# Two unused tiles that move the transposed, gathered and feed-forward rows to other addresses

## The chip, the cores and the metric

The kernel runs on one core of a Trainium2 chip. The metric is the device time of one execution in microseconds (us), as the median of several runs. The engines are named as in the profile: PE is TensorE's matmul, PEld its weight load, DVE is VectorE, ACT is ScalarE, POOL is GpSimd, and SP is SyncE, whose queue issues nearly all loads.

## The reference

The program is a network on one sequence of 256 rows of 1024 numbers, all in float32:

```python
def reference(...):
    x = first_block(x, c, w_ada, ...)
    return second_block(x, positions_2, w_in_2, ...)
```

`first_block` computes a modulation `mod = silu(c) @ w_ada + b_ada`, then `x + g1 * token_mixer(h)` and `x + g2 * relu(h @ w_ff1)**2 @ w_ff2`, where `h` is a normalised and modulated `x`. `token_mixer` multiplies `h` by `w_in` (1024 x 12800), runs retention (4 heads) and dilated attention (12 heads) and merges them with gates and `w_o`. The feed-forward is 4096 wide. `second_block` has two layers. Each one projects `x` by `w_in_2` (1024 x 2488), mixes it (latent attention, mLSTM and a state-space scan), multiplies by `w_out`, and then applies a mixture of 16 experts: `silu(x @ w_gate) * (x @ w_up)` times the share of the expert, times `w_down`, each expert 256 wide.

## The kernel before

Weights come from HBM in chunks of 128 partitions x 1024 numbers (512 KB). A chunk lands in a tile `raw` (or, for experts that are fetched early, `far`). ACT copies it to `whi` in a rounded format (`wsplit`, line 142) and DVE computes the rest, `wlo = raw - whi` (line 145). The activations are split into two parts in the same way. A product is then three matmuls (`mm3`, lines 164 to 168), hi times hi, hi times lo, lo times hi:

```python
def mm3(self, out, l, r, first, last):
    mm = self.nc.tensor.matmul
    mm(out, l[0], r[0], start=first, stop=False)
    mm(out, l[0], r[1], start=False, stop=False)
    mm(out, l[1], r[0], start=False, stop=last)
```

`l` is the operand that is loaded into the array (128 x 128, 512 bytes in each partition), `r` is streamed past it. In the profile each of the three has a row at PEld and one at PE. Two kinds of product matter here.

- Narrow: `proj_tr` loads weights from the ring (`whi`, `wlo`) and streams 256 columns of transposed activations: `h1T` (first block's input), `h2T` (feed-forward input), `rT` (retention's output), `attT`, `xT` (a layer's input).
- Wide: `proj_nat`, `proj_wide` and the experts' `gate_up` and `down` load 128 x 128 pieces of the activations and stream 512 columns of the ring. The activations here are `h1T`, `mT`, `hT`, `xT`, `ffh` (the feed-forward's hidden rows, in blocks of 512), `xg` (the rows that are gathered for the experts) and `ehT` (an expert's hidden rows). In one short stretch at the start of the feed-forward, `fhi` and `flo` from another pool take the place of the ring.

The stages follow each other: modulation and first products (to about 75 us), retention and attention (to about 430), `w_o`, feed-forward (about 475 to 640), and for each layer its mixer and its experts (layer 0's experts from about 800 to 945 us, layer 1's from about 1110 to 1255). The experts run one after another: 24 wide matmuls of gate and up, 12 of down for the expert before, two transposes.

SBUF is laid out by pools, one behind the other in each partition, in the order in which they are opened: `cp` (constants), `ring` (`raw`, `whi`, `wlo`, six of each), `xp` (`x` and the transposed rows `h1T`, `xT`, `mT`, `hT`, `xh`), `sm` (small tiles), and then the pools of a stage, which reuse the room behind `sm`: `pa`/`pr` (retention), `pt` (attention), `pm` (feed-forward: `h2T`, `ffh`, `fhi`, `flo`), `mix` (a layer's mixer), `moe` (experts: `xg`, `ehT`, `far`, `yh`, `PT`). A tile's size in these pools is a multiple of 512 bytes nearly everywhere, so all tiles of a pool have the same remainder modulo 256; behind `moe`'s small `cslot` it changes once more.

Of the kernel before, what the change touches and what calls it, by code (L numbers as in the profile page):

```python
# [10 lines left out]
F32 = mybir.dt.float32  # L11
# [67 lines left out]
class Kern:  # L79
    BANKS = {"mm": "X", "acc": "X", "A": "A", "y": "A", "B": "B", "gu": "B"}  # L80

    def __init__(self, tc, ctx, I, out):
        self.tc, self.nc, self.I, self.out = tc, tc.nc, I, out
        self.ctx = ctx
        self.cp = ctx.enter_context(tc.tile_pool(name="cp", bufs=1))
        self.ring = ctx.enter_context(tc.tile_pool(name="ring", bufs=3))
        self.xp = ctx.enter_context(tc.tile_pool(name="xp", bufs=2))
        self.sm = ctx.enter_context(tc.tile_pool(name="sm", bufs=4))
        self.dp = ctx.enter_context(tc.tile_pool(name="dp", bufs=1, space=DRAM))
        self.n = 0  # L90
        self.pst = None
        self.early = []
        self.gate = self.mark = None
# [2015 lines left out]
```

## Time and profile before

| | us |
|---|---|
| median of 3 runs (1279.0 to 1281.27) | 1281.07 |
| the profiled execution | 1277.76 |
| its span, first to last instruction | 1276.0 |
| PE busy in the span | 1225.8 |
| DVE busy | 954.5 |
| ACT busy | 739.5 |

The profiled execution is one run, and its own time is the one that belongs to the rows below; 1.76 us lie around its span. Matmuls overlap in the records, so the duration of one (about 390 ns for 512 columns) is longer than the time from its start to the next one's start. The second is what a stream costs.

### The profile page before, as it was taken

The page shows a single profiled execution, that of the slowest core. Times are in us where ns is not written, and L with a number is a line of the kernel's source. Part 1 is how long each engine was busy: PE and PEld are TensorE (multiplying, and loading weights), DVE is VectorE, ACT ScalarE, POOL GpSimd, SP SyncE. Part 2 cuts the span into 40 slices and gives each one's busy share as a digit, 9 for nine tenths or more (in the row PEclk, how much of TensorE's full clock was granted, in tenths as well). Part 3 has the DMA queues.
Part 4 walks back from the last instruction along what each step waited for, and adds up shares of the span by engine and source line. Part 5 has one row for each costly group of instructions (what it writes and reads, how often), then busy time and mean ns, then how long its engine had stood idle before and what let it go on. Part 6 is the DMA issues. An engine that isn't in the chain of part 4 may idle for free.

```text
span 1276.0 us, 20435 instructions
## 1 busy us (share of the span) xinstructions
PE 1225.8 (96%) x7528; PEld 1081.3 (85%) x7528; DVE 954.5 (75%) x1647; ACT 739.5 (58%) x1149; POOL 41.1 (3%) x101
## 2 busy tenths in 40 slices
PE   6999999999999999999999999999999999999995
PEld 6888998998999989898888977888879987788884
DVE  6898656565678765555579768899888976889986
ACT  3554344444555654444466663878766756587873
POOL 0000000000000000000010001000001000100000
PEclk8999999999999999999999998999999999899998
DMA  9996564696577556566563522999876342499982
GB/s 283 327 292 199 182 184 146 195 299 199 184 230 255 172 203 197 182 192 188 156 195 106 163 82 75 351 341 350 281 244 218 104 130 70 130 361 339 353 278 93
DMA packets 177170, 271.98 MB, mean 213 GB/s; under 512 B 16363, under 2 KB 109216, under 8 KB 177060
## 3 DMA queue, kind: packets, MB, share of 16 engines
q1 hardware_dynamic: 175252, 265.70, 64.1%
q10 hardware_dynamic: 1296, 3.81, 0.9%
q8 instruction: 61, 1.00, 0.3%
q0 software_dynamic: 512, 1.08, 0.2%
q14 instruction: 49, 0.40, 0.1%
HBM read 268.41 MB, written 2.12 MB: 212 GB/s over the span
## 4 chain that ended last, share of the span: by engine, by line
PE 77%; DVE 11%; DMA 4%; ACT 3%; issue 2%; POOL 1%; SPq 0%; POOLq 0%; ACTq 0%; DVEq 0%
PE ps L167 21%; PE ps L168 21%; PE ps L166 21%; DVE wlo L145 3%; DMA araw<-in_w_ada 2%; PE ps L1652 2%; DVE zc L1178 1%; PE ps L1266 1%; PE ps L1247 1%; DMA raw<-in_w_in 1%; PE ps L1844 1%; DVE ada L384 1%; PE ps L1257 1%; PE ps L1293 1%; PE ps L1814 1%
## 5 line engine op out<-in xcount | busy, mean ns | idle before, releaser
L142 ACT ACTIVATE whi<-raw 128x1024 fp32r<-128x1024 f32 (+3 forms) x348 | 356.6, 1038 | 264.1 <-PE ps L167 152.5
L145 DVE TENSOR_TENSOR wlo<-raw,whi 128x1024 fp32r<-128x1024 f32 x334 | 398.6, 1205 | 147.8 <-ACT whi L142 144.5
L166 PE MATMUL ps<-h1T,whi 128*128 128x256 f32 x576 | 166.4, 289 | 1.7 <-ACT h1T L496 1.7
L167 PE MATMUL ps<-h1T,whi 128*128 128x256 f32 x576 | 165.4, 287 | 0.7 <-DVE h1T L498 0.6
L168 PE MATMUL ps<-h1T,wlo 128*128 128x256 f32 x576 | 165.6, 288 | 0.0
L145 DVE TENSOR_TENSOR wlo<-far,whi 128x1024 fp32r<-128x1024 f32 x100 | 117.9, 1219 | 5.6 <-ACT whi L142 5.4
L142 ACT ACTIVATE whi<-far 128x1024 fp32r<-128x1024 f32 x100 | 103.2, 1056 | 19.2 <-PE ps L168 9.2
L166 PEld LDWEIGHTS ps<-h1T,whi 128*128 128x128 f32 x576 | 111.5, 194 | 3.3 <-ACT h1T L496 2.3
L167 PEld LDWEIGHTS ps<-h1T,whi 128*128 128x128 f32 x576 | 111.7, 194 | 2.2 <-DVE h1T L498 1.4
L168 PEld LDWEIGHTS ps<-h1T,wlo 128*128 128x128 f32 x576 | 111.6, 194 | 0.2 <-DVE wlo L145 0.2
L166 PE MATMUL ps<-whi,xg 128*128 128x512 f32 x256 | 103.7, 405 | 0.0
L167 PE MATMUL ps<-wlo,xg 128*128 128x512 f32 x256 | 101.5, 397 | 0.0
L168 PE MATMUL ps<-whi,xg 128*128 128x512 f32 x256 | 101.4, 396 | 0.0
L384 DVE SCALAR_TENSOR_TENSOR ada<-araw,silu_c,ada 128x512 f32<-128x512 f32 (+1 forms) x88 | 62.4, 713 | 11.8 <-DMA araw<-in_w_ada 9.4
L166 PE MATMUL ps<-h2T,whi 128*128 128x256 f32 x224 | 62.6, 280 | 0.0
L167 PE MATMUL ps<-h2T,whi 128*128 128x256 f32 x224 | 62.6, 279 | 0.0
L168 PE MATMUL ps<-h2T,wlo 128*128 128x256 f32 x224 | 62.5, 279 | 0.0
L168 PEld LDWEIGHTS ps<-whi,xg 128*128 128x128 f32 x256 | 48.1, 188 | 11.3
L167 PEld LDWEIGHTS ps<-wlo,xg 128*128 128x128 f32 x256 | 48.2, 188 | 9.9 <-DVE wlo L145 0.2
L166 PEld LDWEIGHTS ps<-whi,xg 128*128 128x128 f32 x256 | 48.1, 188 | 10.0
L166 PE MATMUL ps<-whi,ffh 128*128 128x512 f32 x128 | 50.7, 396 | 0.0
L167 PE MATMUL ps<-wlo,ffh 128*128 128x512 f32 x128 | 50.6, 396 | 0.0
(513 smaller groups left out, 2878.5 us busy)
## 6 DMA issues: line engine op xcount, KB each, us to landing
raw<-in_w_in SPq DMA_DIRECT2D x124, 512.0 KB, 4.5
raw<-in_w_ff SPq DMA_DIRECT2D x64, 512.0 KB, 3.7
far<-in_w_gate SPq DMA_DIRECT2D x68, 256.0 KB, 5.9
far<-in_w_up SPq DMA_DIRECT2D x68, 256.0 KB, 6.0
araw<-in_w_ada SPq DMA_DIRECT2D x64, 256.0 KB, 5.2
far<-in_w_down SPq DMA_DIRECT2D x32, 512.0 KB, 6.2
raw<-in_w_down SPq DMA_DIRECT2D x32, 512.0 KB, 7.1
raw<-in_w_gate SPq DMA_DIRECT2D x60, 256.0 KB, 5.6
```

Of the source, the lines that this page charges most:

```text
L142: self.nc.scalar.activation(hv, raw, AF.Copy)
L145: self.nc.vector.tensor_sub(lv, raw, hv)
L166: mm(out, l[0], r[0], start=first, stop=False)
L167: mm(out, l[0], r[1], start=False, stop=False)
L168: mm(out, l[1], r[0], start=False, stop=last)
L384: V.scalar_tensor_tensor(acc, raws[k], sc[:, k : k + 1], acc, op0=OP.mult, op1=OP.add)
L1178: V.scalar_tensor_tensor(zc[:, b], xp_[:, i, k : k + 256], cw(k), zc[:, b], op0=OP.mult, op1=OP.add)
L1247: PE.matmul(p[:, t], qT[:, j, t * 128 : t * 128 + 128], kT[:, j], start=True, stop=True)
L1257: PE.transpose(p[:, s, t * 128 : t * 128 + 128], P[:, t, s * 128 : s * 128 + 128], self.ident)
L1266: PE.matmul(p[:, t, j], PTs[j][:, s, t * 128 : t * 128 + 128], v[:, s, h * 64 : h * 64 + 64], start=j == 0 and t == 0 and s == 0, stop=j = ...
L1293: PE.matmul(out(1), Gm[:, 128:256], rhs(full), start=False, stop=False)
L1652: self.nc.tensor.matmul(p[kb // 2][:, kb % 2], xh[i][:, t, kb * 128 : kb * 128 + 128], P[:, t, hf * 256 : hf * 256 + 256], start=t == 0 an ...
```

## The change

Two tiles are added that no instruction writes or reads. They only take room: 48 numbers (192 bytes in each partition) behind the ring, and 56 numbers (224 bytes) in the pool `sm`.

```diff
         self.cp = ctx.enter_context(tc.tile_pool(name="cp", bufs=1))
         self.ring = ctx.enter_context(tc.tile_pool(name="ring", bufs=3))
+        ctx.enter_context(tc.tile_pool(name="line", bufs=1)).tile([128, 48], F32, name="line")
         self.xp = ctx.enter_context(tc.tile_pool(name="xp", bufs=2))
         self.sm = ctx.enter_context(tc.tile_pool(name="sm", bufs=4))
+        self.sm.tile([128, 56], F32, name="line2", tag="line", bufs=1)
         self.dp = ctx.enter_context(tc.tile_pool(name="dp", bufs=1, space=DRAM))
```

On each of the five engines the built program has the same instructions in the same order and with the same waits; only line numbers (two more behind the pads) and addresses differ. These are the addresses that the allocator gives, in bytes within a partition; the remainder modulo 256 is the same for all 128 x 128 pieces of a tile and all blocks of 256 or 512 columns.

| tile | first address before | mod 256 | after | mod 256 |
|---|---|---|---|---|
| `raw`, `whi`, `wlo` (ring) | 27456, 52032, 76608 | 64 | the same | 64 |
| `h1T`, `xT`, `mT`, `hT`, `xh` | 117568 | 64 | 117760 | 0 |
| `x`, `heads`, the first loads of later experts | 101184 | 64 | 101376 | 0 |
| `h2T` | 144480 | 96 | 144896 | 0 |
| `ffh` | 162912 | 96 | 163328 | 0 |
| `fhi`, `flo` | 179296, 191584 | 96 | 179712, 192000 | 0 |
| `rT`, `attT` | 148576, 160864 | 96 | 148992, 161280 | 0 |
| `xg` | 146528 | 96 | 146944 | 0 |
| `araw` (modulation weights) | 171104 | 96 | 171520 | 0 |
| `P` (choice of the gathered rows) | 142432 | 96 | 142848 | 0 |
| `ehT` | 187552 | 160 | 187968 | 64 |
| `far`, `yh` | 191648 | 160 | 192064 | 64 |
| `PT` (experts) | 179360 | 160 | 179776 | 64 |

## Rows read from the trace of the kernel before

**Rows 1.** The page's first part: busy us, share of the span, instructions.

```profile
PE 1225.8 (96%) x7528; PEld 1081.3 (85%) x7528; DVE 954.5 (75%) x1647; ACT 739.5 (58%) x1149; POOL 41.1 (3%) x101
```

**Rows 2.** Windows: length; PE, PEld, DVE, ACT, POOL busy; granted clock; DMA share; GB/s.

```profile
0.00:75.00 75.00, 62.27 (x390) 57.70 (x391) 57.56 (x117) 33.92 (x52) 2.06 (x18) 0.93 0.95 308
480.00:634.00 154.00, 154.00 (x974) 138.16 (x973) 84.49 (x83) 72.79 (x83) 0.00 (x0) 1.00 0.61 184
820.00:900.00 80.00, 80.00 (x354) 64.37 (x353) 74.59 (x79) 64.53 (x79) 0.00 (x0) 1.00 1.03 349
900.00:920.00 20.00, 20.00 (x90) 16.07 (x90) 17.30 (x20) 14.98 (x20) 0.00 (x0) 1.00 0.77 257
```

**Rows 3.** Timeline, PE: start, duration; first and last of 40 in a row.

```profile
312.14 0.39 PE L167 MATMUL ps<-wlo,h1T 128*128 128x512 f32 x1
...
320.98 0.39 PE L167 MATMUL ps<-wlo,h1T 128*128 128x512 f32 x1
```

**Rows 4.** The same, feed-forward's second product, 40 in a row.

```profile
487.24 0.40 PE L167 MATMUL ps<-wlo,ffh 128*128 128x512 f32 x1
...
496.35 0.40 PE L167 MATMUL ps<-wlo,ffh 128*128 128x512 f32 x1
```

**Rows 5.** The same, a narrow product of the first block, 40 in a row.

```profile
349.07 0.28 PE L167 MATMUL ps<-h1T,whi 128*128 128x256 f32 x1
...
353.75 0.28 PE L167 MATMUL ps<-h1T,whi 128*128 128x256 f32 x1
```

**Rows 6.** The same, feed-forward's first product, 40 in a row.

```profile
503.23 0.28 PE L167 MATMUL ps<-h2T,whi 128*128 128x256 f32 x1
...
507.78 0.28 PE L167 MATMUL ps<-h2T,whi 128*128 128x256 f32 x1
```

**Rows 7.** The same, one expert of layer 0, 35 in a row.

```profile
866.24 0.39 PE L167 MATMUL ps<-wlo,xg 128*128 128x512 f32 x1
...
874.17 0.40 PE L168 MATMUL ps<-whi,xg 128*128 128x512 f32 x1
```

**Rows 8.** Groups of PE by form: count, busy us, mean ns of one, idle.

```profile
L167 PE MATMUL ps<-flo,h2T 128*128 128x512 f32 x12 | 4.7, 389 | 0.0
```

**Rows 9.** The same view, one of the three lines of each product.

```profile
L166 PE MATMUL ps<-h1T,whi 128*128 128x256 f32 x576 | 166.4, 289 | 1.7 <-ACT h1T L496 1.7
L168 PE MATMUL ps<-whi,xg 128*128 128x512 f32 x256 | 101.4, 396 | 0.0
L167 PE MATMUL ps<-h2T,whi 128*128 128x256 f32 x224 | 62.6, 279 | 0.0
L167 PE MATMUL ps<-wlo,ffh 128*128 128x512 f32 x128 | 50.6, 396 | 0.0
L168 PE MATMUL ps<-whi,ehT 128*128 128x512 f32 x128 | 50.2, 395 | 0.0
L168 PE MATMUL ps<-whi,h1T 128*128 128x512 f32 x112 | 43.5, 390 | 0.0
L166 PE MATMUL ps<-rT,whi 128*128 128x256 f32 x128 | 36.0, 284 | 0.1
```

**Rows 10.** Timeline, PE, layer 0's mixer: 25 in a row, three shown.

```profile
767.84 0.40 PE L167 MATMUL ps<-wlo,hT 128*128 128x512 f32 x1
...
769.69 0.39 PE L166 MATMUL ps<-whi,hT 128*128 128x512 f32 x1
...
772.86 0.39 PE L168 MATMUL ps<-whi,hT 128*128 128x512 f32 x1
```

**Rows 11.** Groups of DVE by form: count, busy us, mean ns, idle.

```profile
L145 DVE TENSOR_TENSOR wlo<-raw,whi 128x1024 fp32r<-128x1024 f32 x322 | 389.5, 1222 | 147.8 <-ACT whi L142 144.5 <-DMA raw<-in_w_in 1.7 <-issue 0.3
L145 DVE TENSOR_TENSOR wlo<-far,whi 128x1024 fp32r<-128x1024 f32 x100 | 117.9, 1219 | 5.6 <-ACT whi L142 5.4
```

**Rows 12.** Waits of the load queue, 800 to 945 us: total, times, longest.

```profile
SPq L127 <- DVE wlo L145: 29.1, 35, 3.4
```

**Rows 13.** Chain of the first 75 us, shares by line.

```profile
by line: DMA araw<-in_w_ada 18.6%; DMA raw<-in_w_in 10.3%; DVE ada L384 7.7%; PE ps L167 7.0%; DMA raw<-in_p 6.9%; PE ps L166 6.5%; PE ps L168 6.3%; issue 5.2%; DMA c_t<-in_c 5.1%; PE ps L477 4.7%; SPq L127 3.3%; ACT ht L495 2.4%; PE ps L40
```

## The prediction

> **What bounds the kernel now.** The page's first part comes first: TensorE (PE) is busy for 1225.8 of 1276.0 us, and no other engine comes near [rows 1]. An average hides stages, so I cut the span. In the first 75 us PE is busy for 62.27 us while the DMA engines are 95% busy: this stretch waits for transfers. [...]
>
> [...] All the large products are `mm3` matmuls, 512 or 256 columns wide, each with its own weight load. The timeline gives starts; 40 matmuls in a row span 39 spacings.
> - 512 wide, weights from `h1T`, columns from the ring: 8.84 us, so 226.7 ns [rows 3].
> - 512 wide, weights from `ffh`, columns from the ring: 9.11 us, so 233.6 ns (233.3 over longer stretches) [rows 4].
> - 256 wide, weights from the ring, columns from `h1T`: 4.68 us, so 120.0 ns [rows 5].
> - 256 wide, weights from the ring, columns from `h2T`: 4.55 us, so 116.7 ns [rows 6].
>
> The same instruction, the same clock, no waits, and yet two spacings for either width. What differs is the operands' addresses. In the allocator's table `h1T` and the ring both begin 64 bytes past a multiple of 256, while `ffh` and `h2T` begin 96 past one: their two operands stand 32 bytes apart within a 64-byte unit. Equal offsets give 226.7 and 120.0 ns; 32 apart gives 233.3 and 116.7 ns. Equal offsets thus help the wide matmul and hurt the narrow one. An expert (36 wide matmuls in a row, `xg` then `ehT`, 32 or 96 bytes off the ring) has 34 spacings in 7.93 us, 233.2 ns [rows 7]. Two more rows support a relative effect. The tiles `fhi` and `flo` stand at 96 as `h2T` does, so both operands are at 96: their matmuls last 389 ns [rows 8], as those with `h1T` do (390), against 396 with `ffh` [rows 9]. And in layer 0 a run of `hT` matmuls (both at 64) shows the equal-offset stream settling: from 767.84 to 769.69 us eight spacings of 231 ns, then to 772.86 us fourteen of 226.4 [rows 10]. The stream finds the shorter beat after some nine matmuls; streams 32 apart never do.
>
> **The change, part by part.** It adds two tiles that nothing reads or writes. On every engine the same instructions stand in the same order with the same waits; no instruction is added, so the direct cost is nothing. All of it is addresses. After it the ring is still at 64; `h1T`, `h2T`, `xT`, `rT`, `attT`, `mT`, `hT`, `xg`, `ffh` begin at 0, 64 from the ring; `ehT` goes to 64, level with the ring.
>
> The trace has no long stream with operands 64 bytes apart, so that case is bounded from both sides by the two spacings that it does show. I take 64 apart to act as 0 apart. The reason: `xg` and `ffh` (32 below) and `ehT` (96 above) are 128 bytes apart in their distance to the ring, and still last the same (396, 396 and 395 ns [rows 9]), so only the remainder within some small unit counts, and 64 is the smallest unit that fits all rows.
>
> - Experts: 256 x 3 matmuls with `xg` and 128 x 3 with `ehT` [rows 9], which is 36 for each of 32 experts. Two transposes break the stream once per expert. After them I allow 9 spacings at 231 ns [rows 10], a gain of 2.2 each, and 27 that gain 6.5: 195 ns an expert, 6.2 us in all.
> - Feed-forward, second product: 128 x 3 with `ffh` in eight blocks of 48; by the same count 9 x 2.3 + 39 x 6.7 = 281 ns a block, 2.2 us gained.
> - Feed-forward, first product: 224 x 3 with `h2T` go from 116.7 to 120.0: 672 x 3.33 = 2.2 us lost.
> - `rT` (128 x 3 [rows 9]), `attT` (96) and the 128 gather matmuls of line 1652 are of the narrow kind at 32 apart too. 608 x 3.33 = 2.0 us bounds their loss, nothing is the other bound; I take 1.6, as some of them wait for ACT or DVE.
> - `h1T`, `mT`, `hT`, `xT`: 0 apart before, 64 after: no change.
> - Off PE: VectorE's subtraction that reads a raw chunk takes 1222 ns from the ring (offset 64) and 1219 from `far` (160) [rows 11], so I see no cost of an offset there, and price ACT the same way.
>
> Is the gain in the experts covered by something? An expert would need 8.4 us where it needs 8.6. VectorE is busy for 74.59 of 80.00 us in that stretch [rows 2], 93%, which becomes 96%. The transfers: an expert's weights are 3.15 MB, which in 8.4 us are 374 GB/s, above the 349 that the loads reached from 820 to 900 us [rows 2]. But they run ahead: their queue waits for `wlo` to free buffers (29.1 us in 35 waits [rows 12]), and from 900 to 920 us the rate falls to 257 GB/s with PE still full [rows 2]. So I count the gain whole; with that cover gone the experts would stay at their present pace and the sum at -4.6 + 6.2 = 1.6 us lost.
>
> Sum: -6.2 - 2.2 + 2.2 + 1.6 = -4.6 us. The profiled execution took 1277.76 us (span 1276.0), so 1273.2 by its own time. That is 0.36% off; on the median of the runs, 1281.07, it is **1276.5 us**.
>
> [...]
>
> **The rivals.** All use the sums above; "64 apart" is the open quantity.
> 1. *64 apart settles in neither width* (only exactly equal offsets do). Then the narrow matmuls of `h1T` gain: 576 x 3 [rows 9] less some 250 in the transfer-bound first 75 us, 1476 x 3.33 = 4.9 us, and those of `xT` about 0.8. The wide ones that are level now lose: `h1T` and `mT` 432 x 6.7 = 2.9 us, `hT` and `xT` 288 x 3 = 0.9. `xg`, `ffh`, `h2T`, `rT` stay. `ehT` becomes level, but for 12 matmuls between unsettled ones: 9 x 2.2 + 3 x 6.5 = 39 ns an expert, 1.3 us. Net -3.2 us: 1277.9. For it: nothing in the trace shows 64 apart settling.
> 2. *64 apart is best for both* (wide settle, narrow don't). Gains 6.2 + 2.2 + 5.7, no loss: -14.1 us, 1266.9. Against it: wherever the wide ones settle in the trace, the narrow ones do too.
> 3. *64 apart is worst for both; the kernel is slower.* The wide stream does not settle and the narrow ones sit at 120: +3.8 lost on the narrow, +3.8 on the wide ones that are level now, -1.3 for `ehT`: +6.3 us, 1287.4. It turns on one number, the wide spacing at 64 apart: 3.8 - 1.3 = 2.5 us are lost whatever it is, and 1872 wide matmuls that will be 64 apart have a mean spacing of 231.2 ns now (1152 at 233.3, 432 at 226.7, 288 at about 229.7), so the change loses when the new one is above 231.2 - 1.3 = 229.9 ns, about halfway between the two seen.
> 4. *Offsets are not the cause.* Every tile at 96 or 160 also lies high in the partition, far from the ring, and those at 64 lie near it. If distance makes the difference, nothing changes: 1281. For it: distance and offset go together in all the long streams, `fhi` included [rows 8], whose two operands lie near each other. [...]
>
> A last place is the start. `araw`, the modulation weights, goes from 96 to 0, and its transfers are 18.6% of the chain in the first 75 us [rows 13], 14 us. I take nothing from them, the lower bound; a transfer's share that an offset could cost has no row. [...]
>
> **How the numbers follow.** Chances: my forecast 0.42, rival 1 0.14, rival 2 0.08, rival 3 0.16, rival 4 0.20. The forecast alone would lie within 1274 to 1279 (half or all of the narrow losses, and 0.1% for the runs' own spread: 1279.0 to 1281.27). For 8 in 10 the range takes in rivals 1 and 4 whole and stops just short of 2 and well short of 3: 1267 to 1284. About 0.2% (2.6 us) is what a measurement of this kernel can tell from no change. Faster by more: most of the forecast, half of rival 1, rival 2: 0.55. Within: rival 4, the rest: 0.28. Slower: rival 3: 0.17.
>
> **What would show it.** Right: in the changed profile the `ffh` stream of 40 matmuls takes 8.84 us, the experts' 34 spacings 7.75, the `h2T` stream 4.68, and `h1T` streams stay as they are. Rival 1 shows as 4.55 us for `h1T` at 256 columns and 9.11 at 512. Rival 4 shows all four streams as now. The forecast fails if 64 apart has a spacing of its own, or if VectorE's waits appear in the experts and hold PE up.

## The result and the profile after

The changed kernel takes **1266.74 us** (median of 4 runs, 1260.0 to 1269.99), against 1281.17 for the kernel before (4 runs beside them): a ratio of 0.987, 95% interval 0.9838 to 0.9902, which is 12.6 to 20.8 us less. That is faster, and 0.3 us below the predicted range of 1267 to 1284. Its profiled execution took 1267.27 us, with a span of 1265.5.

The page's first part, in the order of [rows 1]:

```profile
PE 1209.6 (96%) x7528; PEld 1070.9 (85%) x7528; DVE 953.9 (75%) x1647; ACT 738.5 (58%) x1149; POOL 41.2 (3%) x101
```

The same counts on every engine. PE is busy for 16.2 us less and its weight loads for 10.4 us less; the other engines differ by at most 1.0 us. The same three stretches as [rows 2], the two later ones moved to where their work now stands:

```profile
0.00:75.00 75.00, 59.70 (x402) 55.48 (x403) 59.01 (x121) 34.34 (x53) 2.06 (x18) 0.95 0.93 315
474.00:628.00 154.00, 154.00 (x981) 139.64 (x981) 85.07 (x84) 72.80 (x83) 0.00 (x0) 1.00 0.61 186
812.00:892.00 80.00, 80.00 (x361) 65.63 (x360) 76.17 (x81) 65.98 (x80) 0.00 (x0) 1.00 1.03 359
```

Feed-forward and experts are still full of PE at a granted clock of 1.00, with 981 matmuls where 974 began, and 361 where it was 354. So the gain is in the spacing. The timeline, 40 in a row each, wide with `h1T` [rows 3], wide with `ffh` [rows 4], narrow with `h1T` [rows 5], narrow with `h2T` [rows 6], and one expert of 35 [rows 7]:

```profile
307.73 0.39 PE L168 MATMUL ps<-whi,h1T 128*128 128x512 f32 x1
...
316.66 0.39 PE L168 MATMUL ps<-whi,h1T 128*128 128x512 f32 x1
...
480.66 0.40 PE L168 MATMUL ps<-whi,ffh 128*128 128x512 f32 x1
...
489.60 0.39 PE L168 MATMUL ps<-whi,ffh 128*128 128x512 f32 x1
...
343.74 0.28 PE L170 MATMUL ps<-h1T,wlo 128*128 128x256 f32 x1
...
348.16 0.28 PE L170 MATMUL ps<-h1T,wlo 128*128 128x256 f32 x1
...
494.73 0.28 PE L170 MATMUL ps<-h2T,wlo 128*128 128x256 f32 x1
...
499.32 0.28 PE L170 MATMUL ps<-h2T,wlo 128*128 128x256 f32 x1
...
859.05 0.40 PE L169 MATMUL ps<-wlo,xg 128*128 128x512 f32 x1
...
866.84 0.39 PE L170 MATMUL ps<-whi,xg 128*128 128x512 f32 x1
```

| stream | before, ns | forecast | after |
|---|---|---|---|
| wide, `h1T` (8.93 us / 39) | 226.7 | 226.7 | 229.0 |
| wide, `ffh` (8.94 / 39) | 233.6 | 226.7 | 229.2 |
| narrow, `h1T` (4.42 / 39) | 120.0 | 120.0 | 113.3 |
| narrow, `h2T` (4.59 / 39) | 116.7 | 120.0 | 117.7 |
| expert, `xg` and `ehT` (7.79 / 34) | 233.2 | 228 | 229.1 |

None of the four values of before that the forecast used comes back in a row whose operands are 64 bytes apart; only `ehT`, level now, settles at 226.7. Operands 64 apart have spacings of their own: 229 wide, and two narrow ones, 113.3 and 117.8, one of which a stream keeps from its start to its end.

Where did the time go? Both traces hold the same PE instructions in the same order, so the time from each matmul's start to the next one's start can be subtracted pair by pair and added up by product (worked out from all starts; in sum 10.6 us between these two executions).

| product | x | forecast, us | measured |
|---|---|---|---|
| narrow with `h1T` | 1728 | 0 | -7.5 |
| narrow with `xT` | 480 | 0 | -0.8 |
| narrow with `rT`, `attT`, gather matmuls (line 1652) | 608 | +1.6 | -0.9 |
| narrow with `h2T` | 672 | +2.2 | +0.7 |
| experts, `xg` and `ehT` | 1152 | -6.2 | -5.3 |
| wide with `ffh` | 384 | -2.2 | -1.5 |
| 512 wide with `h1T`, `hT`, `mT`, `xT` | 720 | 0 | +1.9 |
| all else, in many groups | | 0 | +2.8 |

These rows mix spacing with pauses. Over the pairs that stand back to back in both executions (narrow under 130 ns, wide under 300) the sum is -16.4 us, about what PE's busy time fell by: narrow with `h1T` -8.2 and with `xT` -2.1, the four wide ones with `h1T`, `hT`, `mT`, `xT` +0.8. All other pairs, with pauses or at the lower clock, gave back 5.9 us, 4.1 of them between 75 and 430 us. A faster stream thus did not shorten the kernel by all that it gained.

### The profile page after: what moved, and what is told of

Read it like the earlier page. It is cut to its first block, busy times and chain, and to the rows that moved or that the text cites. A ratio compares the mean times of both kernels' runs of the same rounds, so it can differ in the third digit from the quotient of the medians.

```text
span 1265.5 us, 20435 instructions
## 1 busy us (share of the span) xinstructions
PE 1209.6 (96%) x7528; PEld 1070.9 (85%) x7528; DVE 953.9 (75%) x1647; ACT 738.5 (58%) x1149; POOL 41.2 (3%) x101
## 4 chain that ended last, share of the span: by engine, by line
PE 78%; DVE 12%; DMA 3%; ACT 3%; issue 2%; POOL 2%; SPq 0%; POOLq 0%; DVEq 0%; ACTq 0%
PE ps L169 21%; PE ps L170 21%; PE ps L168 21%; DVE wlo L147 3%; DMA araw<-in_w_ada 2%; PE ps L1654 2%; DVE zc L1180 1%; DVE ada L386 1%; PE ps L1268 1%; DMA raw<-in_w_in 1%; PE ps L1249 1%; PE ps L1846 1%; PE ps L1259 1%; PE ps L1295 1%; PE ps L1816 1%
## 5 line engine op out<-in xcount | busy, mean ns | idle before, releaser
L168 PE MATMUL ps<-h1T,whi 128*128 128x256 f32 x576 | 163.1, 283 | 1.6 <-ACT h1T L498 1.6
L170 PE MATMUL ps<-h1T,wlo 128*128 128x256 f32 x576 | 162.6, 283 | 0.0
L169 PE MATMUL ps<-h1T,whi 128*128 128x256 f32 x576 | 162.0, 281 | 0.1
L168 PEld LDWEIGHTS ps<-h1T,whi 128*128 128x128 f32 x576 | 109.4, 190 | 2.8 <-ACT h1T L498 1.7
L169 PEld LDWEIGHTS ps<-h1T,whi 128*128 128x128 f32 x576 | 109.6, 190 | 1.3 <-issue 0.5
L386 DVE SCALAR_TENSOR_TENSOR ada<-araw,silu_c,ada 128x512 f32<-128x512 f32 (+1 forms) x88 | 62.4, 713 | 10.4 <-DMA araw<-in_w_ada 8.6
L170 PEld LDWEIGHTS ps<-whi,xg 128*128 128x128 f32 x256 | 48.1, 188 | 10.4
```

The source lines that it names most:

```text
L386: V.scalar_tensor_tensor(acc, raws[k], sc[:, k : k + 1], acc, op0=OP.mult, op1=OP.add)
```

## The experiments

Theory A, read from the changed kernel's profile, is that the distance between the two operands of a matmul (address of the streamed columns minus address of the weights, modulo 256) sets the spacing, and 64 apart has a spacing of its own. Against it stood B, the forecast's assumption (64 apart acts as level, that is, as 0 apart); C, that a tile is read faster when it begins at a multiple of 256, whatever the other operand does; and rival 4, the position alone. In the kernel the distance is 64 or -64 (that is, 192) by whether a tile is the columns or the weights. Every kernel is the one before with pads of other sizes at the places of the diff.

**The second pad alone.**

```diff
         self.sm = ctx.enter_context(tc.tile_pool(name="sm", bufs=4))
+        self.sm.tile([128, 56], F32, name="line2", tag="line", bufs=1)
```

> The second pad alone. h1T and xT stay level with the ring (64); the stage pools go to 64 too, level with the ring; ehT goes to 128, 64 from it. No large tile is at a multiple of 256. Theory A (the distance between the two operands sets the spacing, and 64 apart has spacings of its own, read from the changed kernel: 229 ns wide, 113.3 or 117.8 ns narrow): h1T 120.0 and 226.7 as before; xg and ffh go from 233.3 to 226.7, h2T and rT from 116.7 to 120.0, ehT to 229. By the terms -6 for xg and ffh, -1.6 for ehT, +2.2 for h2T, +1.6 for rT and attT: about 1277.5. Theory B (64 acts as level, my forecast): ehT 226.7, otherwise the same, 1276.5. Theory C (a tile runs faster at multiples of 256 bytes): nothing gained, 1281.

Measured 1277.67 us, ratio 0.9971 (0.9954 to 0.9989), where A's terms sum to 0.997. The timeline of this run, feed-forward's second product:

```profile
486.13 0.40 PE L167 MATMUL ps<-whi,ffh 128*128 128x512 f32 x1
...
495.00 0.39 PE L167 MATMUL ps<-whi,ffh 128*128 128x512 f32 x1
```

8.87 us, 227.4 ns (226.7 in its second half), with `ffh` at 64, no multiple of 256, and level with the ring. `h2T`, level too, went to 119.9. C falls for the stage tiles: they take the level spacings without any alignment. What B said of level operands is right, too.

One term missed: `ehT`, the weights here, stands 64 above the ring, so that columns minus weights is 192, and A had 229 for it. One expert's 12:

```profile
865.93 0.40 PE L167 MATMUL ps<-whi,ehT 128*128 128x512 f32 x1
...
868.50 0.39 PE L169 MATMUL ps<-whi,ehT 128*128 128x512 f32 x1
```

2.57 us for 11 spacings, 233.6 ns, hardly below the 234 of before: its 1.6 us did not come, and that the sum fits so well is in part luck. It is the first sign that the two sides differ.

**The first pad alone.**

```diff
         self.ring = ctx.enter_context(tc.tile_pool(name="ring", bufs=3))
+        ctx.enter_context(tc.tile_pool(name="line", bufs=1)).tile([128, 48], F32, name="line")
```

> The first pad alone. h1T, xT, mT and hT go to 0, 64 from the ring; the stage pools go to 32, so xg, ffh, h2T and rT stay 32 from the ring and ehT goes from 96 to 32. Theory A: h1T and xT narrow 113.3 or 117.8 where they were 120.0, a gain of about 8 us, less 2.3 us for their wide streams at 229; the stage's streams stay at 233.3 and 116.7: about 1275.5. Theory B (64 acts as level): nothing changes, 1281. Theory C (multiples of 256): h1T gains in both widths, the stage none: 1271 to 1274.

Measured 1277.12, ratio 0.9963 (0.9946 to 0.998), against A's 1275.5 (0.996). B's "nothing changes" falls. Narrow with `h1T`, 40 in a row:

```profile
302.78 0.28 PE L168 MATMUL ps<-h1T,whi 128*128 128x256 f32 x1
...
307.20 0.28 PE L168 MATMUL ps<-h1T,whi 128*128 128x256 f32 x1
```

That is 113.3 ns. In streams of 30 or more, `h1T` and `xT`, 0 apart before and 64 now, give 113.4 to 113.9 or 117.8 narrow, and `h1T` and `mT` 228.9 to 229.9 wide, while the wide streams with `ffh` stay at 233.3. `h2T`, now 32 below the ring where it was 32 above, went from 116.7 to 118.3: the sign of a distance counts here too.

**Every distance of the change, no multiple of 256.** The diff of the change, and ahead of the ring:

```diff
+        ctx.enter_context(tc.tile_pool(name="fore", bufs=1)).tile([128, 16], F32, name="fore")
         self.ring = ctx.enter_context(tc.tile_pool(name="ring", bufs=3))
```

> The changed kernel with a pad of 64 bytes ahead of the ring: every distance between operands as in the changed kernel, but the ring at 128 and the large tiles at 64, none at a multiple of 256. Theory A (only the distance counts): the changed kernel's time, 1260 to 1270, with its spacings (229 wide, 113.3 or 117.8 narrow, ehT 226.7). Theory C (multiples of 256): the gain is gone, about 1281.

Measured 1268.62 (1267.21 to 1270.16), ratio 0.99 (0.9863 to 0.9936): the whole gain within the interval. Wide with `ffh` and narrow with `h1T`, 40 in a row each:

```profile
482.50 0.39 PE L169 MATMUL ps<-whi,ffh 128*128 128x512 f32 x1
...
491.43 0.39 PE L169 MATMUL ps<-whi,ffh 128*128 128x512 f32 x1
...
334.77 0.28 PE L171 MATMUL ps<-h1T,wlo 128*128 128x256 f32 x1
...
339.19 0.28 PE L171 MATMUL ps<-h1T,wlo 128*128 128x256 f32 x1
```

229.0 and 113.3 ns, as in the changed kernel. C falls altogether.

**Pads of 256 bytes at both places.**

```diff
+        ctx.enter_context(tc.tile_pool(name="line", bufs=1)).tile([128, 64], F32, name="line")
...
+        self.sm.tile([128, 64], F32, name="line2", tag="line", bufs=1)
```

> Two pads of 256 bytes at the same two places: the tiles move further than in the change (256 and 512 bytes), but every address keeps its remainder. Theory A and C: no change, 1281 (1279 to 1282), with 226.7 and 120.0 at h1T, 233.3 at ffh, 116.7 at h2T. Rival 4 (how far apart the tiles lie, not their remainders): some of the gain shows, under 1275.

Measured 1279.74, ratio 0.9995 (0.9971 to 1.0018): no change clear of noise, with the spacings of `ffh` (233.3) and narrow `h1T` (120.0) as before; of the narrow streams 32 apart, one of `h2T` and one of `rT` sat at 117.8 where before they had 116.7. Rival 4 falls: the move of 192 bytes took narrow `h1T` from 120.0 to 113.3 or 117.8, and here 256 bytes left it at 120.0 and 512 left `ffh` at 233.3.

**Bare streams.** What a distance costs, by itself: a kernel of nothing but matmuls, with no wait between them and no other engine at work.

```python
def run(d, n, count):
    for a in range(count // 3):
        g = ps[a // 8 % 2][:, :n]
        for c, (w, m) in enumerate(((0, 0), (0, 1), (1, 0))):
            at = d // 4 + w * 2048 + a % 8 * 128
            co = m * 4096 + a % 8 * n
            nc.tensor.matmul(g, W[:, at : at + 128], M[:, co : co + n], ...)
...
for d in plan:
    run(d, 256, 96)
    run(d, 512, 48)
```

> A kernel of nothing but steady streams: 96 matmuls of 256 columns and then 48 of 512 for each of eighteen distances d, in the order of mm3 (weights hi, hi, lo; columns hi, lo, hi), with no wait between them. The columns start 64 bytes past a multiple of 256, the weights d bytes further on; the model of the reference is left out and its output is only a copy of sums. Theory A (the distance alone sets the spacing): at d 0 120.0 and 226.7 ns, at 32 118.3 and 233.3, at 224 116.7 and 233.2, at 64 narrow 113.3 or 117.8, at 192 wide 229; 96, 128 and 160 have no row yet, by B they repeat 32, 0 and 32. Theory B (what counts is the distance within 64 bytes, as the forecast had it): 64, 128 and 192 read like 0. Theory D (the spacing comes from what the other engines and transfers do at the same time, not from the operands): one spacing for each width at all distances.

> The kernel of steady streams once more, with the distances in reversed order and every tile 64 bytes lower, so that the columns start at a multiple of 256; its output is again only a copy of sums. If the distance alone counts, every spacing is that of the first such run at the same distance, but narrow at 192, which may come out at 113.3 or 117.8 in any place. If an address of its own counts (a multiple of 256), the table changes as a whole.

Windows of the first of these runs (length; PE busy and matmuls; granted clock; DMA share; GB/s): a narrow and a wide stream with columns minus weights at 0, the same at 224, a narrow one at 192, and another at 192 much later:

```profile
36.60:46.60 10.00, 10.00 (x85) 1.00 0.00 0
48.20:58.20 10.00, 10.00 (x46) 1.00 0.01 2
59.00:69.00 10.00, 10.00 (x87) 1.00 0.00 0
70.40:80.40 10.00, 10.00 (x44) 1.00 0.00 0
81.40:91.40 10.00, 10.00 (x91) 1.00 0.01 2
...
327.80:337.80 10.00, 10.00 (x88) 1.00 0.01 2
```

85 to 91 narrow matmuls, and 44 or 46 wide ones, fit into the same 10 us at the same clock. In the code `d` is how far the weights lie behind the columns, so columns minus weights is 256 - d (`run(64, 256, 96)` is the narrow stream at 192, as with `h1T` in the changed kernel, and `run(192, 512, ...)` the wide one at 64). From the starts of the second half of each stream in both runs, in ns:

| columns minus weights | narrow | wide |
|---|---|---|
| 0 | 120.0 | 226.7 |
| 32 | 116.7 or 117.8 | 233.3 |
| 64 | 117.8 | 228.9 |
| 96 | 120.0 | 233.3 |
| 128 | 118.6 | 233.3 or 232.1 |
| 160 | 117.3 or 118.6 | 234.2 |
| 192 | 113.3 or 117.8 | 233.3 |
| 224 | 118.3 | 233.3 |
| 176 / 208 | 118.7, 118.8 / 118.3, 117.8 | 231.9, 232.1 / 233.3 |
| 240 / 248 | 118.3 / 115.5 | 226.7 or 233.3 / 230.5 |

The second run had its columns at multiples of 256 and the distances in the other order, and gives the same table but for the entries with two values: A holds, C is out once more, and so is D, that the other engines or the transfers make the spacing. B fails in its root: 64, 128 and 192 do not read like 0, and from 64 to 192 it is the sign that decides (wide 228.9 and 233.3). Where two values stand, one stream has the one and another the other.

**The changed kernel once more**, without any edit.

> The changed kernel once more, unaltered, for a second profiled execution. If the state of a narrow stream 64 apart (113.3 or 117.8 ns) is chosen anew in each execution, the seven feed-forward streams with h2T, which were all at 117.8, come out otherwise in some place (1260 to 1270, as its runs lay); if the program fixes it, the same streams are at 117.8 again.

Measured 1265.33 (1262.19 to 1268.95), ratio 0.9874 (0.9839 to 0.9909). The timeline of its profiled execution (1262.19 us, span 1260.4), narrow with `h2T`:

```profile
469.73 0.28 PE L168 MATMUL ps<-h2T,whi 128*128 128x256 f32 x1
...
474.15 0.28 PE L168 MATMUL ps<-h2T,whi 128*128 128x256 f32 x1
```

4.42 us for 39, 113.3 ns, where the first execution had 117.8 in all seven streams; here all seven had 113.5 or 113.6. `h2T` costs 2.0 us less than before in place of 0.7 more. So it is not the program that fixes it; this alone is 2.8 us of the 5.1 between the two profiled executions.

**The stage pools alone, at the changed kernel's own remainders modulo 256.**

```diff
+        self.sm.tile([128, 40], F32, name="line2", tag="line", bufs=1)
```

> A second pad of 160 bytes alone: the stage pools go to 0 and ehT to 64, as in the changed kernel, while h1T, xT, mT and hT stay at 64, level with the ring. Theory A (the table of steady streams by distance): xg and ffh 229, ehT 226.7, h2T and rT 113.3 or 117.8, h1T 120.0 and 226.7. By the two profiles' difference over the same instructions: experts -5.3, ffh -1.5, rT and attT -0.8, h2T between -2.1 and +0.7: 1272 to 1275. If the two halves are not independent, or the gain hangs on h1T, it is near 1280 or near 1267.

Measured 1268.85 (1266.07 to 1273.56), ratio 0.9902 (0.9877 to 0.9928): more than expected. By the pair-by-pair difference, `xg` gave 2.9, `ehT` 2.5, `ffh` 1.6, `h2T` 2.1, `rT` 1.3 and `attT` 0.4 us, 10.7 in sum: here all narrow stage streams but one of 25 matmuls were at or close to 113.4, the better of their two values, where the estimate had taken `rT` from the changed kernel's first execution, with half of it at 117.8. The ratio is worth 12.5 us; the 1.8 beyond that sum have no shown term. With the first pad alone, 0.0037 below 1, and this one, 0.0098, the halves add up to 0.9865, the change's 0.987. Its profiled execution was its slowest, 1273.56, and shows what else differed, in the second layer's mixer:

```profile
1040.00:1100.00 60.00, 55.94 (x310) 46.92 (x308) 39.82 (x112) 29.85 (x75) 6.48 (x12) 0.91 0.19 62
```

The granted clock is 0.91 over these 60 us, with PE busy for 55.94 of them; it was 0.95 there in the profiled execution of the changed kernel; in the kernel before it was 1.00 there and 0.94 from 1050 to 1110 us.

**96 apart.**

```diff
+        ctx.enter_context(tc.tile_pool(name="line", bufs=1)).tile([128, 24], F32, name="line")
...
+        self.sm.tile([128, 56], F32, name="line2", tag="line", bufs=1)
```

> Pads of 96 and 224 bytes: the rows and the stage tiles all at 160, 96 past the ring, ehT at 224. Theory A, from the steady streams (columns minus weights 96: 120.0 narrow; 160: 234.2 wide): h2T loses 672 x 3.3 = 2.2, rT and attT 1, the wide streams with h1T, mT, hT and xT 720 x 6.5 = 4.7, xg and ffh 1152 x 0.9 = 1.0, h1T narrow and ehT nothing: +9, about 1290, slower than before by the same kind of edit. If steady streams apart from the kernel don't tell its time: within 0.3% of before.

Measured 1288.0 (1284.33 to 1291.95), ratio 1.006 (1.0034 to 1.0086): slower than before by 0.6%, where the table of bare streams foretold 0.7%. Wide with `h1T` in this run:

```profile
309.54 0.39 PE L168 MATMUL ps<-whi,h1T 128*128 128x512 f32 x1
...
318.67 0.39 PE L168 MATMUL ps<-whi,h1T 128*128 128x512 f32 x1
```

9.13 us, 234.1 ns, against 226.7 [rows 3]; `h2T` had 120.0. Those spacings came as foretold; how close the sum came is in part luck. In the profiled execution the wide streams with `h1T`, `hT`, `mT`, `xT` cost 3.3 us more where 4.7 were foretold, and those with `xg` and `ffh` 3.7 in place of 1.0, most of it with `xg` while PE was full at a granted clock of 0.94 from 800 to 830 us and 0.96 from 1120 to 1160 (1.00 in both before). The same kind of edit, tiles that nobody uses, moves the kernel to either side of 1281.

**64 apart on the other side of the ring.**

```diff
+        ctx.enter_context(tc.tile_pool(name="line", bufs=1)).tile([128, 16], F32, name="line")
...
+        self.sm.tile([128, 56], F32, name="line2", tag="line", bufs=1)
```

> Pads of 64 and 224 bytes: the rows and the stage tiles at 128, again 64 bytes from the ring but on its other side, ehT at 192. Theory A with the sign (columns minus weights 64: narrow 117.8 always; 192: wide 233.3): h1T narrow -3.8, xT -0.8, h2T +0.7, the wide streams with h1T, mT, hT and xT 720 x 6.5 = +4.7, xg and ffh none: +0.8, about 1281 to 1282. Theory A without a sign (64 apart is 64 apart): the changed kernel's 1260 to 1270.

Measured 1279.47, ratio 0.9991 (0.9972 to 1.001): the gain is gone, and the sign is what the change got right. Narrow and wide with `h1T`:

```profile
334.79 0.28 PE L169 MATMUL ps<-h1T,whi 128*128 128x256 f32 x1
...
339.38 0.28 PE L169 MATMUL ps<-h1T,whi 128*128 128x256 f32 x1
...
305.71 0.39 PE L168 MATMUL ps<-whi,h1T 128*128 128x512 f32 x1
...
314.81 0.39 PE L168 MATMUL ps<-whi,h1T 128*128 128x512 f32 x1
```

117.7 and 233.3 ns. Not quite "117.8 always": four of the narrow streams had 113.3.

**What comes before a narrow stream.**

```python
for d in plan:
    run(d, 512, 48)
    run(64, 256, 96)
for c in (36, 39, 42, 45, 48):
    run(192, 512, c)
    run(64, 256, 96)
for d in plan:
    run(d, 256, 48)
    run(64, 256, 96)
```

> Steady streams again, to see what sets a narrow stream at distance 64 to 113.3 or to 117.8 ns: 21 such streams of 96 matmuls, eight behind 48 wide matmuls at each of the distances 0 to 224, five behind 36 to 48 wide ones at one distance (192, that of ffh in the changed kernel), eight behind 48 narrow ones at each distance. The output is only a copy of sums. If the operands that came just before choose the state (their distance or their number), both values appear among the 21, and a stream keeps its value to its end. If it is left to the execution as a whole, all 21 come out alike. If a stream drifts from one to the other, its two halves differ.

Windows of two narrow streams at 192, behind wide ones at 0 and at 224 (columns as in the first bare run):

```profile
48.80:58.80 10.00, 10.00 (x87) 1.00 0.01 2
71.40:81.40 10.00, 10.00 (x91) 1.00 0.01 2
```

Both values appear, and both halves of every stream agree. Behind a wide stream at 0, 128 or 160, and behind a narrow one at 0, at 224 or at 192 itself with 117.8, the value was 117.8: six of the 21. In the 15 others it was 113.3. The stream before seems to hand the state on, and a wide stream at 64 seems to pass on that of the narrow one before it: all six such streams here, of whatever length, had 113.3 on both sides, and in each of the two earlier bare runs one had 117.8 on both (the narrow one ahead of it was at 64 there). That is what the seven `h2T` streams do, which stand between wide streams with `ffh` and were all alike in either execution. What puts the first of them there in one execution and not in the other stays open: the pauses ahead of it were not controlled. One narrow stream at 64, behind one at 192 with 113.3, had 113.3 here, so 64 has both values, too.

## Why the prediction was wrong

**What bounds the kernel: right.** In feed-forward and experts PE is full at a granted clock of 1.00, for 154.00 of 154.00 and 80.00 of 80.00 us, before [rows 2] and after, and there the spacing of matmuls is the kernel's time. Addresses set it: pads alone moved the kernel.

**The failing step** is "I take 64 apart to act as 0 apart". Its reason was that `xg`, `ffh` and `ehT` last the same, "so only the remainder within some small unit counts". (It calls them 128 bytes apart in their distance to the ring; by the table of addresses all three lie above it, by 32 and 96, which is 64 apart.) But these were wide matmuls only, for which the table of bare streams has 233.3 at 32, 96, 192 and 224 and 234.2 at 160. That they nearly agree there says nothing of 64, where the wide one has 228.9, or of the narrow ones. The prediction did name this way of failing, a spacing of its own for 64 apart, but had no rival for it.

The trace of before also had a sign that a narrow stream is not settled by its distance alone. Two streams with `rT`, 32 apart, 40 in a row each:

```profile
169.83 0.28 PE L166 MATMUL ps<-rT,whi 128*128 128x256 f32 x1
...
174.42 0.28 PE L166 MATMUL ps<-rT,whi 128*128 128x256 f32 x1
...
228.81 0.28 PE L168 MATMUL ps<-rT,wlo 128*128 128x256 f32 x1
...
233.36 0.28 PE L166 MATMUL ps<-rT,whi 128*128 128x256 f32 x1
```

117.7 and 116.7 ns; the prediction took 116.7 for all of them.

**The terms.** The step sized all of them by the two spacings of before. Between the two profiled executions the miss is 6.0 us (-10.6 for -4.6), between the medians 9.8.
- `h1T`, `mT`, `hT`, `xT`, "no change": -8.3 us narrow, +1.9 wide. This net -6.4 is about the whole miss of 6.0, since the misses of the other terms happen to cancel, +0.4 in sum.
- `h2T` +2.2: +0.7 in one execution, -2.0 in another. `rT`, `attT` and line 1652, +1.6: -0.9. Narrow streams 64 apart are never at 120.0. Line 1652 is another case: its `P` and `xh` are both at 0 after the change, so level, and its back-to-back spacings did rise, from 117.3 to 119.6 ns on the mean, though its 128 matmuls as a whole changed by less than 0.1 us.
- Experts -6.2: -5.3. Right in place, a little small: `xg` is at 229 and not 226.7 after its transposes, and `ehT`, level now, has 227.4 on the mean.
- `ffh` -2.2: -1.5, by 229 in place of 226.7; the kernel with the second pad alone, level, gave 2.2.
- The cover held: VectorE is busy for 76.17 of 80 us (95%), the loads reach 359 GB/s, and PE is still full, so the experts took their gain whole. Elsewhere the forecast had no term for pauses, and they gave back 5.9 us.

**The rivals.** Rival 2's time, 1266.9, is nearly what came, but its mechanism is only half right: 64 apart, on the side that the change took, is better than 32 apart for the wide one (229 for 233.3) and best for the narrow one where it has 113.3 (117.8 is no better than 116.7), but level operands are best for the wide one. I had given it 0.08, because wherever wide streams settle in the trace the narrow ones sit at 120; that rested on level operands alone. Rival 1 is wrong (`h1T` narrow gains, but to 113.3, and `xg` gains too). Rival 3 is wrong for this change; a slower kernel came with another pad, 96 apart, by 0.6%. Rival 4 was tried and fell.

The bare streams have 113.3 to 120.0 and 226.7 to 234.2 ns at one granted clock, 1.00, with a DMA share of 0.01 at most in the windows shown: here the distance of the two operands sets the spacing. By what mechanism it does so stays open.

**The start**, priced at nothing, stays without a shown term. In the first 75 us the loads moved 315, 321 and 317 GB/s with `araw` at 0 (the changed kernel twice, and the stage pools alone), 308 and 311 at 96 (before, and the pads of 256), 316 at 160, 313 at 128, 303 and 312 at 64 and 300 at 32. These are single executions, and 160 does as well as 0. What an offset costs a transfer, no run here isolates.

**The range** stopped short of rival 2, and held the chance of two spacings only. The faster kernel had the largest chance, 0.55.

## What to carry to other kernels

Where PE is full, read the spacing of starts in each steady stream, and with it the distance of the two operands' addresses modulo 256: at one shape and clock it was worth 6% narrow (113.3 to 120.0 ns) and 3% wide (226.7 to 234.2) here, in streams of this number format with a weight load for each matmul; no run has another kind. A case that the trace doesn't show is not one of the two that it does; a kernel of bare streams gave the whole table in one run of 447 us, and that table then foretold that another pad makes the kernel slower (1.007, measured 1.006). Edits that only move tiles took this kernel to ratios from 0.987 to 1.006, and a comparison of two such kernels should keep the distances.

## What the runs showed of the hardware

- The spacing depends on the sign of the distance: wide 228.9 ns at 64 and 233.3 at 192, narrow 116.7 or 117.8 at 32 and 118.3 at 224.
- A narrow stream 64 apart has two lasting values, 113.3 and 117.8 ns. In the bare streams the value went with the stream before, and between executions of one program it can differ (`h2T`: 117.8 in all seven streams of one, 113.5 or 113.6 in another).
- Multiples of 256 bytes were worth nothing by themselves: with the ring and all tiles behind it 64 bytes further on the gain was the same within the intervals (0.99 against 0.987).
- From the table, a kernel with `ffh` level and all else as changed should gain 0.7 us more (2.2 in place of 1.5). It wasn't run, since the changed kernel's runs differ by 10 us.
